# The cost that a build-time clock gives a matmul of the weight stream

## The chip, the cores and the metric

The kernel runs on one core of a Trainium2 chip. The metric is the device time of one execution, in microseconds. A core has five engines with queues of their own: TensorE (PE in the profile, its weight loads PEld), VectorE (DVE), ScalarE (ACT), GpSimd (POOL) and SyncE (SP), which here issues nearly all DMAs. An engine takes its instructions in the order in which the program has them, and waits where one of them needs what another engine has not done yet. The order of the instructions on each queue is therefore part of the program, and it is all that is changed here.

## The reference

One step of a layer of a hybrid decoder, for 256 prompt tokens and 8 sequences of 8 new tokens, 320 tokens in all, in float32:

```python
hn = rmsnorm(x, p['norm1'])
proj = hn @ p['w_in']                       # 2048 x 12752
y_s5 = s5_mixer(...)                        # diagonal state space, a scan over the tokens
y_rw = rwkv7_mixer(...)                     # a 64 x 64 state for each of 8 heads
y_gd = gdn_mixer(...)                       # gated delta rule, a 128 x 128 state for each of 8 heads
merged = (jax.nn.sigmoid(gt_s5) * (y_s5 @ p['w_br_s5'])
          + jax.nn.sigmoid(gt_rw) * (y_rw @ p['w_br_rwkv'])
          + jax.nn.sigmoid(gt_gd) * (y_gd @ p['w_br_gdn']))
x = x + merged @ p['w_out']
up = rmsnorm(x, p['norm2']) @ p['ffn_w_up'] # 2048 x 11264
up_c, n_ffn = causal_dwconv(up, ffn_conv, p['ffn_conv_w'])
gate, val = jnp.split(up_c + p['ffn_conv_b'], 2, axis=-1)
x = x + (jax.nn.silu(gate) * val) @ p['ffn_w_down']
```

The new states of the mixers and convolutions are outputs too, and x is normed once more at the end.

## The kernel before

*The weight stream.* All 320 tokens stand on the free axis, channels on the partitions. The weights come in 530 steps of 512 KB each (`plan`, line 2024): eight tiles of 128 x 128. Float32 accuracy is had from TensorE's faster format (F32R) by splitting: every weight tile w becomes a high part `whi` (ACT rounds it) and a low part `wlo` (DVE takes the difference), four tiles of 128 columns at a time (128 x 512), and the inputs are split in the same way. Each tile of a step is then three matmuls of 128 x 128 by 320 columns (`products`, line 554): whi with the input's high part, whi with its low part, wlo with its high part. This text calls them a triple. 530 steps are 4,240 triples, 12,720 weight matmuls. The splits are issued up to two steps ahead of their use.

*The tasks.* Everything else is written as generators, the tasks: first norm, S5, delta net (`gdn_main`, `gdn_prompt`, `gdn_sample`), RWKV (`rw_main`), the evacuation of PSUM banks, convolutions, gates. Their matmuls are ordinary float32 ones, most of them small: 64 columns, or 32 x 32 blocks in the inverses of triangular matrices (`tri_inverse`, line 1145, which sends blocks out to DRAM and back by DMA in another layout). A task issues one hop of instructions, then yields; its next hop may be issued when the inputs are held to be ready. S5 must end before the delta net begins, and the delta net before RWKV; RWKV must end before its branch's weights are due.

*What sets the order.* While the program is built, a `Clock` (line 112) keeps an estimated time for each engine. Each instruction is given a cost (`pe_cost` line 229, `dve_cost`, `act_cost`, `pool_cost`), and begins when its engine is free and its operands are ready, with a latency between engines (line 115). The chip does not see this clock; it only decides where instructions are put. After each triple, `poll` (line 531) lets tasks issue hops until the clock of PE has gone on by BURST = 500 ns; a hop in progress is not cut. `able` (line 522) says whether a task may go: its inputs must be ready at the time of PE's clock less 100 ns, free PSUM banks must be there, the DVE and ACT that it uses may be at most LEAD = 2100 ns ahead of PE's clock (double that for the first norm), and a task that uses PE must wait while the heat is negative. The heat (line 209) is a running balance: each matmul adds its columns (times 4 for float32, times its share of the 128 rows) and takes away PACE = 1.1 for each ns of PE's clock; it is capped at HEAT = 700. If no task may go, `split_some` (line 445) splits a part of the weights where ACT or DVE is not more than IDLE = 300 ns ahead of PE's clock. `finish` (line 542) lets tasks go on without the stream where a step needs their result.

The cost of a float32 matmul in the build-time clock is 5 + 1.667 ns for each of the larger of its columns and its weights' columns (line 233), and that of a pair of matmuls in different column groups is less. POOL's tensor_tensor of n elements a row costs 102 + 2.25 n ns (line 253), which the first norm uses to scale its 16 tiles (line 639).

Of the kernel before, what the change touches and what calls it, by code (L numbers as in the profile page):

```python
# [94 lines left out]
class Carve:  # L95
    """Pieces of one flat tile, one after the other."""
# [15 lines left out]
class Clock:  # L112
    """Estimates when each instruction runs, from the order of issue and what it reads and writes."""
# [24 lines left out]
    def after(self, eng, by, t):  # L138
        """When eng can go on after what another one did up to t."""
        return t if eng == by == "pe" or not t else t + self.LAT[by]  # L140

    def known(self, key):
        """What was done to a tile; a new one has to wait for those that had its place."""
        return self.mem.setdefault(key, [[(0, 1 << 20, 0, 1 << 40), self.freed, "dve", 0.0, "dve"]])
# [70 lines left out]
def run(ap):  # L215
    """Elements in a row of memory."""
    n = 1
    for s, c in reversed(ap.ap[ap.space != "DRAM":]):
        if s != n and c > 1:
            break  # L220
        n *= c
    return n
# [6 lines left out]
def pe_cost(name, outs, ins, a, k):  # L229
    n = free_size(outs[0])  # L230
    if ins[0].dtype == F32R:
        return 2.7 + n / 2.4
    return 5 + 1.667 * max(n, free_size(ins[0]) if name == "matmul" else ins[0].shape[0], 32)
# [28 lines left out]
class Engine:  # L262
    """An engine whose instructions the clock follows."""
# [36 lines left out]
class Task:  # L300
    """A generator that issues one hop of instructions after the other. It yields what the next hop waits for: a number of
    PSUM banks, or a condition."""
# [4 lines left out]
    def place(self):  # L307
        """Where it goes on."""
        g = self.gen
        while g.gi_yieldfrom is not None:  # L310
            g = g.gi_yieldfrom
        return g.gi_code, g.gi_frame.f_lineno


class Kernel:
# [43 lines left out]
    # ---- small helpers  # L359
# [9 lines left out]
    def bank(self, shape=(128, T)):  # L369
        """A free PSUM bank, as a tile of that shape."""  # L370
        i = self.spare.pop(0)
        n = int(np.prod(shape[1:]))
        a = self.banks[i][0:shape[0], 0:n]
        if len(shape) == 2:
            return a
        names = "abcd"[:len(shape) - 1]
        return a.rearrange("p (%s) -> p %s" % (" ".join(names), " ".join(names)), **dict(zip(names[1:], shape[2:])))
# [13 lines left out]
    def rstd_of(self, ms, out, tmp, twice=False):  # L391
        """1 / sqrt(ms + eps), with a Newton step after the tables; or -2 times that."""
        act, tt = self.nc.scalar.activation, self.nc.vector.tensor_tensor
        act(out, ms, AF.Ln, bias=self.eps)
        act(out, out, AF.Exp, scale=-0.5)
        tt(tmp, out, out, op=OP.mult)
        self.nc.vector.scalar_tensor_tensor(out=tmp, in0=ms, scalar=self.eps, in1=tmp, op0=OP.add, op1=OP.mult)
        if twice:
            self.nc.vector.scalar_tensor_tensor(out=out, in0=tmp, scalar=-3.0, in1=out, op0=OP.add, op1=OP.mult)
            return  # L400
        self.nc.vector.tensor_scalar(tmp, tmp, -0.5, 1.5, op0=OP.mult, op1=OP.add)
        tt(out, out, tmp, op=OP.mult)

    def halves(self):
        """Two parts of every tile of a matrix."""
        hi = self.mid.tile([128, KD, T], F32R, tag="hh", name="high")
        return [(hi[:, k], self.mid.tile([128, T], F32R, tag="hl%d" % k, name="low")) for k in range(KD)]

    # ---- the stream of weights
# [12 lines left out]
    def room(self):  # L422
        """How many parts of the weights may be split by now."""
        return self.PARTS * min(self.at + self.SPL_BUFS, len(self.steps))
# [20 lines left out]
    def split_some(self):  # L445
        """Splits a part where an engine has nothing to do."""
        c = self.clock.t
        if self.ns < self.nh and c["dve"] <= c["pe"] + self.IDLE:
            n, s = self.part(self.ns)
            if self.clock.written(self.split_t[n][0][:, s]) <= max(c["dve"], c["pe"]) + self.NEAR:  # L450
                self.split_low()
                return True
        if self.nh < min(self.room(), self.ns + self.AHEAD) and c["act"] <= c["pe"] + self.IDLE:
            self.split_high()
            return True
        return False

    def split_to(self, n):
        """Splits at least n parts."""
        while self.ns < min(n, self.PARTS * len(self.steps)):  # L460
            self.split_low()
        while self.nh < min(n + self.EARLY, self.room()):
            self.split_high()

    # ---- tasks beside it
# [19 lines left out]
    def spawn(self, gen, now=False, rank=2):  # L485
        """A task; those of low rank go first."""
        t = Task(gen, rank)
        self.tasks.insert(sum(u.rank <= rank for u in self.tasks), t)
        if now:
            self.hop(t)  # L490
        return t
# [8 lines left out]
    def par(self, *gens):  # L500
        """Generators side by side."""
        ts = [self.spawn(g) for g in gens]
        yield lambda: self.ended(*ts)

    def fetches(self, bufs, source):
        """Loads into a ring of buffers, each when what its buffer had is no longer needed."""
# [11 lines left out]
    def wait(self, *aps):  # L518
        """The next hop waits for these."""
        self.clock.end = max([self.clock.end] + [self.clock.written(a) for a in aps])  # L520
# [10 lines left out]
    def poll(self):  # L531
        """Lets the tasks issue what is ready to run."""
# [21 lines left out]
    def products(self, o, h, l, s, rhs, first, last):  # L554
        """Adds the products of some weight tiles, from number s on, with the pairs in rhs to the bank o."""
# [9 lines left out]
    # ---- first norm, input projection  # L565
# [40 lines left out]
    def prep(self, i):  # L606
        """Pair i of the input's tiles times the norm's weights, in two parts."""
# [3 lines left out]
    def norm1(self):  # L611
        """The factors of the tokens; the first columns are scaled by them afterwards, the others' input here."""
# [31 lines left out]
    def first_step(self, i):  # L644
        """Two tiles of the input for all of the first four columns."""
# [34 lines left out]
    def turn(self, ring, size, gen):  # L680
        """Starts a generator that uses the next of a ring's buffers, when the ones before have left it."""
# [7 lines left out]
    def evac(self, dst, p, r, parts=slice(None)):  # L689
        """A column of the projection out of PSUM; times the tokens' factors, if it came without."""  # L690
# [39 lines left out]
    # ---- gated delta net  # L730
# [52 lines left out]
    def head_norm(self, h):  # L783
        """Sums of a head's squares, key's and query's."""
# [7 lines left out]
    def gdn_main(self):  # L792
# [7 lines left out]
        # rows: one value per head and token  # L800
# [47 lines left out]
        # rows to all partitions, through DRAM  # L848
# [5 lines left out]
        # rows to tokens on partitions  # L854
# [17 lines left out]
        # value and key rows, tokens on partitions  # L872
# [22 lines left out]
        # products of keys with keys and queries inside a chunk  # L895
# [61 lines left out]
        # norm over the head, gate  # L957
# [27 lines left out]
    def gdn_prompt(self, s, ot, vt, kt, tk, yt, at, egl):  # L985
        """Chunk after chunk, the state in s."""
# [55 lines left out]
    def gdn_sample(self, shs, kqs, res, ot, vt, kt, tk, yt, at, egl):  # L1042
        """One state for each sequence and head, read once for the products and once for the update."""
# [64 lines left out]
        # both parts of keys and values, four blocks of rows for the four products  # L1108
# [36 lines left out]
    def tri_inverse(self, nt, halves, name, tw, tx, tt):  # L1145
        """(1 - n)^-1 in place of every 64 x 64 block n of nt (strictly upper; rows on partitions 64 hf + r, then groups of
        eight blocks); halves lists (hf, number of groups)."""
# [66 lines left out]
    # ---- S5  # L1214
    def pexp(self, x, out, new):
        """exp, to float32's accuracy."""
# [212 lines left out]
    def glu_step(self, ch):  # L1429
        """Columns 2 ch and 2 ch + 1 of the gate."""  # L1430
# [28 lines left out]
    # ---- RWKV  # L1459
# [39 lines left out]
    def rw_main(self):  # L1499
# [87 lines left out]
        # tokens on partitions  # L1587
# [37 lines left out]
        def solve(c, ws, first):  # L1625
            """uv of chunk c, from the states' part that first() adds."""
# [132 lines left out]
        # group norm, bonus, gate  # L1759
# [43 lines left out]
    # ---- branches and gates  # L1803
    def gate(self):
        """The next gate of the branches, or the next column of the input that the output projection adds to."""
# [53 lines left out]
    # ---- output projection, second norm's factors  # L1859
# [56 lines left out]
    # ---- feed forward  # L1916
# [26 lines left out]
    def ff_col(self, i, j, p):  # L1943
        """A column of the up projection: norm's factors, convolution; with the second of a pair, their product."""
# [29 lines left out]
    def down_step(self, g, cols, k0, n, last):  # L1974
        """n tiles from k0 on for each of the columns."""
# [32 lines left out]
    def end(self):  # L2008
        """The last norm; its factors come out times -2."""
# [62 lines left out]
def pack_w(w):  # L2072
    """Pieces of 8 x 128 rows by 128 columns."""
    k, c = w.shape
    return np.ascontiguousarray(w.reshape(k // 1024, 8, 128, c // 128, 128).transpose(3, 0, 2, 1, 4))


def pack_pairs(w):
    """Pieces of 4 x 128 rows by two times 128 columns."""
# [7 lines left out]
def device_inputs(inp):  # L2087
# [43 lines left out]
    def rw_cols(v):  # L2131
        """(..., RWKV columns) as 16 tiles of 128"""
# [39 lines left out]
def host_outputs(o):  # L2172
    """The device's arrays, channels first, in the reference's layouts."""
# [28 lines left out]
```

## Time and profile before

| what | us |
| --- | --- |
| runs before (device time) | 2127.69, 2132.31, 2140.75 |
| median | 2132.31 |
| profiled execution, from the first to the last instruction (span) | 2151.2 |
| PE busy | 2126.8 |
| DVE busy | 1368.1 |
| ACT busy | 1024.0 |
| POOL busy | 246.4 |
| mean granted TensorE clock | 0.973 |

The profiled execution has no other time of its own than its span; that lies 18.9 us above the median of the three runs. Durations below are those of the profiled execution.

How to read it: a row of the weight stream names the PSUM bank that is written and the operands, so `bank<-high,whi` is a matmul of the input's high part with a weight's high part. The name of the input tells the stage: xg and high are the first projection (from 5.6 and 72.4 us), yg, ys, yr the branches (from 892.5 us), high once more the output projection (from 1093.5 us), x2h and x2l the up projection (from 1206.2 us), hidh and hidl the down projection. All instructions are recorded under one line, L283, since one helper issues them; so one goes by the names. A float32 matmul leaves two records. The matmul records overlap: one begins before the one ahead of it has ended, so the distance of their starts, not their duration, is what one costs.

### The profile page before, as it was taken

What the parts mean: (1) busy time and instruction counts of PE and PEld (TensorE: products, weight loads), DVE (VectorE), ACT (ScalarE), POOL (GpSimd) and SP (SyncE); (2) the same over time, 40 slices, a digit from 0 to 9 for tenths busy, and PEclk for the clock granted to TensorE, in tenths of its full rate; (3) what the DMA queues carried; (4) which work ended last, traced back from release to release, by engine and by line L of the source; (5) the groups of instructions that cost most, each with busy time, mean ns of one, the idle gap of its engine ahead of it and who ended that gap; (6) DMA issues with size and microseconds to landing.
All of it is one profiled execution on the core that took longest, in us unless ns stands there. A gap on an engine that the chain in (4) does not pass through costs nothing.

```text
span 2151.2 us, 37239 instructions
## 1 busy us (share of the span) xinstructions
PE 2126.8 (99%) x14557; PEld 2042.6 (95%) x14557; DVE 1368.1 (64%) x2535; ACT 1024.0 (48%) x1932; POOL 246.4 (11%) x467
## 2 busy tenths in 40 slices
PE   8999999999999999999999999999999999999997
PEld 8999999999789999977999999999999999999997
DVE  7979898776238665714875666666644466666444
ACT  6666666653224765322444444444433344444443
POOL 2311101200000000000000122222200022222000
PEclk9999999999979999958999999999999999999999
DMA  6574555566317664623665544444444444444543
GB/s 230 193 250 146 160 171 172 161 205 198 134 45 254 226 204 135 201 83 92 212 200 177 162 147 151 149 152 148 153 150 147 150 153 148 147 151 151 165 149 106
DMA packets 131825, 351.05 MB, mean 163 GB/s; under 512 B 27024, under 2 KB 53184, under 8 KB 131392
## 3 DMA queue, kind: packets, MB, share of 16 engines
q1 hardware_dynamic: 130752, 345.56, 50.7%
q0 software_dynamic: 752, 3.10, 0.4%
q8 instruction: 114, 1.87, 0.3%
q14 instruction: 63, 0.52, 0.1%
q10 hardware_dynamic: 144, 0.01, 0.0%
HBM read 319.55 MB, written 29.06 MB: 162 GB/s over the span
## 4 chain that ended last, share of the span: by engine, by line
PE 97%; DVE 1%; DMA 1%; ACT 0%; issue 0%; SPq 0%; DVEq 0%; ACTq 0%
PE bank L283 97%; DVE low L283 0%; DVE wlo L283 0%; DMA x<-rdx 0%; DMA rdy<-triw 0%; DVE xf L283 0%; SPq L283 0%; DMA vec<-vec 0%; DMA x<-gdx 0%; ACT rstd L283 0%; DVE triw L283 0%; DVE squares L283 0%; DVE ev L283 0%; ACT whi L283 0%; DVE acc L283 0%
## 5 line engine op out<-in xcount | busy, mean ns | idle before, releaser
L283 ACT ACTIVATE whi<-wraw 128x512 fp32r<-128x512 f32 x1060 | 620.9, 624 | 765.1 <-issue 455.1
L283 DVE TENSOR_TENSOR wlo<-wraw,whi 128x512 fp32r<-128x512 f32 x1060 | 709.8, 694 | 382.7 <-ACT whi L283 373.3
L283 PE MATMUL bank<-high,whi 128*128 128x320 f32 x1728 | 550.5, 319 | 0.0
L283 PE MATMUL bank<-low,whi 128*128 128x320 f32 x1728 | 533.5, 309 | 0.0
L283 PE MATMUL bank<-high,wlo 128*128 128x320 f32 x1728 | 533.5, 309 | 0.0
L283 PE MATMUL bank<-x2h,whi 128*128 128x320 f32 x1408 | 435.3, 309 | 0.0
L283 PE MATMUL bank<-x2l,whi 128*128 128x320 f32 x1408 | 435.1, 309 | 0.0
L283 PE MATMUL bank<-x2h,wlo 128*128 128x320 f32 x1408 | 435.1, 309 | 0.0
L283 PEld LDWEIGHTS bank<-high,whi 128*128 128x128 f32 x1728 | 325.0, 188 | 23.0 <-issue 16.4
L283 PEld LDWEIGHTS bank<-low,whi 128*128 128x128 f32 x1728 | 325.6, 188 | 2.2
L283 PEld LDWEIGHTS bank<-high,wlo 128*128 128x128 f32 x1728 | 325.7, 188 | 0.0
L283 PEld LDWEIGHTS bank<-x2l,whi 128*128 128x128 f32 x1408 | 264.3, 188 | 0.1
L283 PEld LDWEIGHTS bank<-x2h,whi 128*128 128x128 f32 x1408 | 264.3, 188 | 0.1
L283 PEld LDWEIGHTS bank<-x2h,wlo 128*128 128x128 f32 x1408 | 264.3, 188 | 0.0
L283 PE MATMUL bank<-hidl,whi 128*128 128x320 f32 x704 | 216.5, 308 | 0.0
L283 PE MATMUL bank<-hidh,wlo 128*128 128x320 f32 x704 | 216.5, 307 | 0.0
L283 PE MATMUL bank<-hidh,whi 128*128 128x320 f32 x704 | 216.5, 307 | 0.0
L283 POOL COPY blk<-blk 128x62 f32<-128x62 f32 x88 | 63.5, 722 | 627.7 <-DVE blk L283 627.7
L283 PEld LDWEIGHTS bank<-hidh,whi 128*128 128x128 f32 x704 | 131.9, 187 | 0.0
L283 PEld LDWEIGHTS bank<-hidh,wlo 128*128 128x128 f32 x704 | 131.9, 187 | 0.0
L283 PEld LDWEIGHTS bank<-hidl,whi 128*128 128x128 f32 x704 | 131.9, 187 | 0.0
L283 DVE TENSOR_TENSOR blk<-bank,rstd 128x320 f32<-128x320 f32 x88 | 43.3, 492 | 104.0 <-PE bank L283 104.0
(332 smaller groups left out, 2301.3 us busy)
## 6 DMA issues: line engine op xcount, KB each, us to landing
wraw<-w_in SPq DMA_DIRECT2D x192, 512.0 KB, 4.0
wraw<-w_up SPq DMA_DIRECT2D x176, 512.0 KB, 3.6
wraw<-w_down SPq DMA_DIRECT2D x80, 512.0 KB, 3.6
wraw<-w_out SPq DMA_DIRECT2D x32, 512.0 KB, 3.4
shs<-gst SPq DMA_DIRECT2D x16, 512.0 KB, 3.9
wraw<-w_br_g SPq DMA_DIRECT2D x16, 512.0 KB, 3.7
gates<-ev SPq DMA_DIRECT2D x48, 160.0 KB, 1.8
gt<-gates SPq DMA_DIRECT2D x48, 160.0 KB, 4.2
```

Of the source, the lines that this page charges most:

```text
L283: return f(*a, **k)
```

## The change

One constant in the build-time clock's cost of TensorE's instructions. A matmul of the stream's format costs 13.2 ns beside its columns, where it cost 2.7 ns; for 320 columns 146.5 instead of 136.0. The costs of the float32 matmuls and of all other instructions stay. The rest of the diff takes out docstrings and comments and leaves every line where it was.

```diff
 def pe_cost(name, outs, ins, a, k):
     n = free_size(outs[0])
     if ins[0].dtype == F32R:
-        return 2.7 + n / 2.4
+        return 13.2 + n / 2.4
     return 5 + 1.667 * max(n, free_size(ins[0]) if name == "matmul" else ins[0].shape[0], 32)
```

The cost enters PE's estimated time (lines 206 to 210), and by it everything that compares with PE's clock: `begin`, `ended`, `able`, `poll`, `split_some`, and the heat. The instructions, their number, their operands and the buffers are the same; where the tasks' instructions and the splits stand in the queues is set anew by the program that builds the kernel.

## The prediction

> **What bounds the kernel now.** I read the profile page first (span, busy times, clock, chain, costliest groups), then the windows of some stretches, the waits, the chain in order of time, and the timeline of the two stages in which the clock falls.
>
> ```profile
> span 2151.2 us, 37239 instructions
> PE 2126.8 (99%) x14557; PEld 2042.6 (95%) x14557; DVE 1368.1 (64%) x2535; ACT 1024.0 (48%) x1932; POOL 246.4 (11%) x467
> ...
> PEclk9999999999979999958999999999999999999999
> ...
> PE 97%; DVE 1%; DMA 1%; ACT 0%; issue 0%; SPq 0%; DVEq 0%; ACTq 0%
> ...
> L283 ACT ACTIVATE whi<-wraw 128x512 fp32r<-128x512 f32 x1060 | 620.9, 624 | 765.1 <-issue 455.1
> L283 DVE TENSOR_TENSOR wlo<-wraw,whi 128x512 fp32r<-128x512 f32 x1060 | 709.8, 694 | 382.7 <-ACT whi L283 373.3
> ```
>
> TensorE (PE) carries 97% of the chain that ended last, and is busy for 99% of the span. No other engine is near: DVE 64%, ACT 48%. So the time is the sum of the matmuls at the granted clock, plus the little time in which PE waits. The clock row has two dips, near the middle.
>
> ```profile
> PE bank L283 <- ACT whi L283: 5.6, 1, 5.6
> PE bank L283 <- DVE wlo L283: 4.8, 3, 2.6
> PE bank L283 <- DMA x<-rdx: 0.7, 1, 0.7
> ```
>
> These are all the waits of PE that the profile shows: 11.1 us, of which 5.6 us is the first weight tile at the start. A better order can win back hardly anything here. What is left is the clock:
>
> ```profile
> 525.00:640.00 115.00, 114.89 (x864) 91.90 (x863) 28.45 (x74) 25.60 (x51) 0.54 (x1) 0.85 0.31 104
> ...
> 915.60:983.90 68.30, 68.30 (x540) 52.82 (x537) 9.54 (x18) 12.85 (x27) 1.46 (x5) 0.50 0.22 68
> 1080.00:2106.00 1026.00, 1026.00 (x6996) 1025.84 (x6995) 614.57 (x1057) 447.12 (x830) 158.73 (x270) 1.00 0.50 155
> ```
>
> In these rows the columns are: stretch, its length, busy time and count of PE, PEld, DVE, ACT, POOL, then granted clock. Half of the kernel, 1080 to 2106, runs at clock 1.00 with PE always busy: 1026.00 / 6996 = 146.7 ns per weight matmul. In the delta net's stage (525 to 640) the clock is 0.85, that is 2 x 0.15 x 115 = 34.5 us at half speed; in RWKV's stage 68.3 us stand at 0.50.
>
> **The change part by part.** One constant changes: line 232 gives a weight matmul of 320 columns 13.2 + 133.3 = 146.5 ns in the build-time clock instead of 2.7 + 133.3 = 136.0. The row above says 146.7, so the new figure is the right one. The instructions and their number stay. What moves is where the tasks' instructions are issued between the weight matmuls: while the build-time clock waits X for a task's input it now issues X / 146.5 weight matmuls rather than X / 136.0, 7.2% fewer.
>
> *The dense half, 1080 to 2106.* PE is never idle, tasks there issue almost no matmul, and DVE is busy 614.57 of 1026 us. Moving DVE and ACT work a few hundred ns earlier costs nothing; the cover is the weight tiles split up to two steps ahead. Taken as 0.
>
> *The two stages with small matmuls.* Does the new constant change how densely they lie? After every three weight matmuls (products, line 554) poll may issue tasks until 500 ns of PE time have been given out. If something is always ready, every triple is followed by one such hop, whatever a weight matmul is held to cost.
>
> ```profile
> 561.54 0.42 PE L283 MATMUL bank<-high,whi 128*128 128x320 f32 x1
> ...
> 562.09 0.33 PE L283 MATMUL bank<-kq,gs 128*128 128x64 f32 x2
> 562.35 0.43 PE L283 MATMUL bank<-at,vn 64*128 64x64 f32 x2
> 562.71 0.43 PE L283 MATMUL bank<-kq,gs 128*128 128x64 f32 x2
> 563.08 0.43 PE L283 MATMUL bank<-at,vn 64*128 64x64 f32 x2
> 563.44 0.41 PE L283 MATMUL bank<-high,whi 128*128 128x320 f32 x1
> ...
> 567.22 0.47 PE L283 MATMUL bank<-high,whi 128*128 128x320 f32 x1
> ...
> 570.32 0.63 PE L283 MATMUL bank<-high,whi 128*128 128x320 f32 x1
> ```
>
> A hop is 8 records here (an f32 matmul leaves two). The windows of the weight tiles alone, high parts first and low parts second, give the triples:
>
> ```profile
> 525.00:640.00 115.00, 40.82 (x139) 23.18 (x138) 11.54 (x18) 9.70 (x16) 0.85 0.31 104
> ...
> 525.00:640.00 115.00, 23.12 (x69) 14.70 (x69) 11.54 (x18) 0.85 0.31 104
> ```
>
> 139 + 69 = 208 weight matmuls are 69 triples; the other 864 - 208 = 656 records are 9.5 to each triple, one hop. So this stage is saturated, and so is RWKV's, where 540 records stand in 68.3 us. The second brake is the build-time heat (line 209): a triple earns 3 x (320 - 1.1 x 146.5) = 476 now, 511 before; the hop shown (costs 218 each, columns 256 and 128) earns 2 x 16 - 2 x 112 = -192. The balance stays positive, so this brake closes neither before nor after. Hence the density, and with it the half-clock time, stays about as it is. What half clock costs: the same triple and hop takes 563.44 - 561.54 = 1.90 us at full clock and 570.32 - 567.22 = 3.10 us at half; in RWKV's stage 3.57 against 2.11 us:
>
> ```profile
> 967.10 0.90 PE L283 MATMUL bank<-ys,whi 128*128 128x320 f32 x2
> ...
> 970.67 0.90 PE L283 MATMUL bank<-ys,whi 128*128 128x320 f32 x2
> ...
> 990.07 0.56 PE L283 MATMUL bank<-yg,whi 128*128 128x320 f32 x2
> ...
> 992.18 0.56 PE L283 MATMUL bank<-yg,whi 128*128 128x320 f32 x2
> ```
>
> With no half clock at all the stages would be 34.5 x (1 - 1.90/3.10) = 13.4 us and 68.3 x (1 - 2.11/3.57) = 27.9 us shorter: 41.3 us, the most that can be won. With the delta net's stage all at half clock its other 80.5 us would grow by 80.5 x (3.10/1.90 - 1) = 50.8 us. These are the ends for this term.
>
> *The waits for the triangular inverses.* Their blocks go out and come back by DMA, and the order covers that with weight matmuls.
>
> ```profile
> 520.84 0.34 SPq L283 DMA_DIRECT2D gates<-ev  x1
> ...
> 527.27 365.45 PE bank L283 x2521
> ...
> 897.95 0.32 SPq L283
> ...
> 905.32 6.47 DMA x<-rdx
> ...
> 911.84 1224.30 PE bank L283 x8468
> ```
>
> From the first SP issue of the chain to PE's going on are 6.4 us at the first and 13.9 us at the second, where PE already waited 0.7 us (row above). With 7.2% fewer weight matmuls as cover PE comes 0.5 and 1.0 us sooner and waits that much longer: +1.5 us, between 0 and, were the whole transfer bare, 6.47. Behind that wait stands the whole weight stream. The idle time comes just ahead of small matmuls, so I add one more stretch of 3.4 us (the dip's shortest unit, 34.5 us being some ten of them) at half clock in the delta net's stage: 3.4 x 0.39 = +1.3 us; its ends are the -41.3 and +50.8 above.
>
> *The first norm.* POOL scales 16 tiles while DVE splits them:
>
> ```profile
> 44.82 17.97 POOL L283 TENSOR_TENSOR x_sb<-x_sb,rstd 128x320 f32<-128x320 f32 x16 [29.89 <-ACT whi L283]
> ...
> L283 DVE SCALAR_TENSOR_TENSOR low<-x_sb,vec,high 128x320 fp32r<-128x320 f32 x14 | 13.8, 1028 | 0.0
> ```
>
> The build-time clock holds POOL's 16 at 822 ns each, 13.2 us, hence 97 weight matmuls before and 90 now. Seven fewer are 1.0 us less cover, and they need 0.6 of a low part of 0.69 us less: +0.6 us, between 0 and the 4.8 us that PE waits there now.
>
> *All other hops.* Outside these stretches 133 groups of small matmuls stand in the stream, from the first to the last of these rows:
>
> ```profile
> 127.89 0.73 PE L283 MATMUL bank<-csq,msk 128*32 128x320 f32 x4
> ...
> 1042.19 0.70 PE L283 MATMUL bank<-tn,mskr 128*128 128x320 f32 x2
> ```
>
> A typical wait ahead of one is an ACT pass and two DVE passes, 0.62 + 2 x 0.69 = 2.0 us (an estimate from the page's groups), so each comes up to 7.2%, 0.14 us, sooner against its input: at most 133 x 0.14 = 19 us. At the least 0; a gain is excluded, since PE shows no wait on a task's DVE or ACT work that could go. Tasks are only asked once a triple (0.44 us), which covers most of 0.14: I take a tenth, +1.9 us.
>
> *Sum.* 1.5 + 1.3 + 0.6 + 1.9 = +5.3 us. The profiled execution has a span of 2151.2 us and would come to 2156.5; it lies 18.9 us above the median of the timed runs, 2132.31. Against that median: 2137 us, +0.2%.
>
> **A rule against the change.** The rows give 146.7 ns per weight matmul. The Trainium skill, "TensorE: Matmul & The Clock Gate", section "Wait — 56ns, not 53.3ns?", puts back-to-back matmuls at N / 2.4 GHz + 2.5 ns, which would be 135.8 ns here, what the old constant holds. By it the new constant would make every hop too early, and the last term would stand at its end: 2132 + 19 + 3 = 2154 us. The trace disagrees by 11 ns.
>
> **The rivals.** (1) *Nothing moves that counts:* all hops stay covered, 2132 us. For it speaks that PE waits for no task now; against it that one DMA wait is already bare by 0.7 us.
> (2) *Slower, the clock:* the later DMA data at 527 us lets the clock fall at once, and the delta net's stage stays at half speed. For it: at 915.6 us the fall came right behind such a wait and lasted 68.3 us with PE busy throughout. Against it: in the same profile the first wait, at 527, was followed by full clock. All of the stage at half: 2132 + 51 = 2183 us. It decides from 21 us on, when 21 / 0.63 = 33 of the 80.5 us go over to half clock.
> (3) *Faster, the clock:* other neighbours for the small matmuls keep RWKV's stage at full speed. The span less 41.3 us is 2110 us, and no run can go lower by the clock alone; that is 22 us under the median. Against it: the stage is saturated, so its density hardly depends on the constant. The Trainium skill, same page, section "Why this matters for your kernels", says that the clock stays up if PE has no gaps over about 3 us. By that rule this rival would be sure, as the longest wait after the start is 2.6 us; the trace disagrees, with PE busy 68.30 of 68.30 us at clock 0.50.
>
> **How the numbers follow.** A measurement here can tell about 1%, 21 us, from no change. The small cost summed above: 0.59. Rival 1: 0.16; both end within 1%: 0.75. Rival 2 and late hops beyond 21 us: 0.15. Rival 3: 0.10. The time is that of the likeliest, 2137. The range takes in 19 us of late hops with the small terms (2154) and a small part of rival 2 above, and a 20 us gain of rival 3 below: 2112 to 2160, leaving out about 2 in 10.
>
> **What would show it.** In the changed profile: 146.7 ns per weight matmul in the dense half, as now; PE's wait for x<-rdx 1 to 2 us rather than 0.7, and one of about 0.5 us for x<-gdx; about 9.5 other records per triple in the delta net's stage; about 100 us at half clock in the two stages. A much larger or smaller half-clock time makes the prediction wrong, and so does a new wait of PE on DVE of over 10 us in the S5 stage, where DVE has the least room.

## The result

The changed kernel takes 2168.3 us in the median of four runs (2161.24 to 2173.6), against 2131.48 us before. The ratio is 1.0152, with a 95% interval from 1.0104 to 1.02: slower by about 1.5%, outside the predicted range. The same program once more, beside later kernels, gave 1.014 (1.0098 to 1.0182). The profiled execution is one of the four runs, 2161.24 us, with a span of 2159.5 us.

From the page of the changed kernel:

```profile
span 2159.5 us, 37235 instructions
PE 2115.3 (98%) x14557; PEld 2032.7 (94%) x14557; DVE 1360.2 (63%) x2535; ACT 1011.4 (47%) x1919; POOL 244.6 (11%) x467
...
PEclk9999999997899998999999999999999999999999
...
PE 84%; DVE 9%; DMA 3%; ACT 2%; issue 1%; SPq 0%; DVEq 0%; POOL 0%; ACTq 0%
```

The instructions are the same, and this execution even had less half-clock time than the profiled one of before (a mean clock of 0.980 against 0.973). But PE's share of the chain that ended last has fallen from 97% to 84%; DVE, DMA and ACT now stand in it. The chain in order of time was 130 pieces long and is now 799: again and again it leaves PE for the work that PE waits for. All waits of PE (us in total, times, longest):

```profile
PE bank L283 <- DVE wlo L283: 5.8, 4, 2.9
PE bank L283 <- ACT whi L283: 5.8, 1, 5.8
PE bank L283 <- DMA x<-rdx: 4.6, 1, 4.6
PE bank L283 <- DMA x<-gdx: 3.6, 1, 3.6
PE bank L283 <- DVE m L283: 3.0, 7, 0.9
PE bank L283 <- ACT csq L283: 2.3, 3, 1.1
PE bank L283 <- issue: 1.3, 1, 1.3
PE bank L283 <- ACT tp L283: 1.2, 1, 1.2
PE bank L283 <- DMA g<-rkv: 1.0, 1, 1.0
PE bank L283 <- DVE squares L283: 0.9, 1, 0.9
PE bank L283 <- DVE stacked L283: 0.7, 1, 0.7
```

They are 30.2 us, where they were 11.1: 19.1 us more. The first two, the start and the first norm, were there before, and so were 0.7 us of the wait for x<-rdx. The rest is new, and nearly all of it waits for the tasks: the two inverses, S5's output (m), the delta net's head norm (csq), RWKV's inputs.

The window of the delta net's stage, then two stretches at half clock, one at its start and one at the start of RWKV's small matmuls, then the dense half:

```profile
487.00:604.00 117.00, 114.23 (x854) 91.89 (x854) 27.54 (x72) 26.12 (x51) 0.54 (x1) 0.84 0.32 105
...
490.80:511.30 20.50, 20.50 (x181) 16.87 (x181) 1.99 (x3) 6.97 (x16) 0.00 (x0) 0.50 0.33 119
842.40:873.10 30.70, 28.09 (x309) 23.70 (x309) 2.16 (x4) 7.66 (x17) 1.47 (x5) 0.50 0.34 94
1090.00:2115.00 1025.00, 1025.00 (x6989) 1024.84 (x6988) 605.31 (x1053) 450.30 (x828) 158.59 (x270) 1.00 0.51 155
```

The dense half is what it was: 1025.00 / 6989 = 146.7 ns per weight matmul. The delta net's stage has 854 records in 117 us, against 864 in 115: nearly as dense, and at nearly the same clock, 0.84 against 0.85. What differs is where half clock begins. The timeline of PE (start, length, idle time before it in brackets) at the two inverses:

```profile
485.82 0.30 PE L283 MATMUL bank<-high,wlo 128*128 128x320 f32 x1
489.75 0.95 PE L283 MATMUL bank<-x,nt 32*32 32x32 f32 x32 [3.62 <-DMA x<-gdx]
...
840.14 0.31 PE L283 MATMUL bank<-high,wlo 128*128 128x320 f32 x1
845.01 1.91 PE L283 MATMUL bank<-x,gm 32*32 32x32 f32 x32 [4.56 <-DMA x<-rdx]
```

PE stands still for 3.62 us and 4.56 us with weight matmuls behind it in its own queue that need nothing. Half clock lasts from 490.8 to 511.3, right behind the first of these waits, and from 842.4 to 873.1, beginning within the second.

How much is waiting and how much is clock? Each run has its span and granted clock c, so its half-clock time is h = 2 (1 - c) x span. Lines fitted through the runs give span = 2102 + 0.42 h for before (81 runs, mean h 71 us) and 2125 + 0.41 h for the changed kernel (10 runs, mean h 91 us). So some 23 us are time that is there at full clock too, and 0.41 x 20 = 8 us are clock (the difference of the two means, 20 us, is uncertain by some 9, the 8 us by some 4). Below, the time at full clock is a kernel's mean span less 0.42 of its mean h.

### The profile page after: what moved, and what is told of

Same layout as the page of the kernel before. It is cut to its first block, busy times and chain, and to the rows that moved or that the text cites. A ratio compares the mean times of both kernels' runs of the same rounds, so it can differ in the third digit from the quotient of the medians.

```text
span 2159.5 us, 37235 instructions
## 1 busy us (share of the span) xinstructions
PE 2115.3 (98%) x14557; PEld 2032.7 (94%) x14557; DVE 1360.2 (63%) x2535; ACT 1011.4 (47%) x1919; POOL 244.6 (11%) x467
## 4 chain that ended last, share of the span: by engine, by line
PE 84%; DVE 9%; DMA 3%; ACT 2%; issue 1%; SPq 0%; DVEq 0%; POOL 0%; ACTq 0%
PE bank L283 84%; DVE wlo L283 3%; DVE m L283 1%; DVE t L283 1%; DVE conv L283 1%; ACT whi L283 1%; DVE bu L283 1%; DVE low L283 1%; DMA wraw<-w_in 0%; SPq L283 0%; DMA o_wkvs<-chain 0%; DMA x<-rdx 0%; DMA wraw<-w_u 0%; ACT tp L283 0%; DMA gdy<-triw 0%
## 5 line engine op out<-in xcount | busy, mean ns | idle before, releaser
L283 DVE TENSOR_TENSOR wlo<-wraw,whi 128x512 fp32r<-128x512 f32 x1060 | 701.1, 694 | 389.2 <-ACT whi L283 380.2
L283 PE MATMUL bank<-high,whi 128*128 128x320 f32 x1728 | 560.9, 325 | 0.0
```

Source lines behind the costliest of these rows:

```text
L283: return f(*a, **k)
```

## The experiments

Theory A: the loss is cover. The new constant puts fewer weight matmuls over every task chain, 7.2% by the arithmetic; the build-time clock holds these chains shorter than the chip takes, and the old, too small constant made up for that. Rival B: the loss is half-clock time that the small matmuls bring about by themselves. Rival C: another arrangement by chance, with no trend. The heat balance is no rival: in building the two programs it is below zero after 53 and 54 of 13,712 matmuls, and holds back no hop in either.

**More of the same.** The constant from 13.2 to 24.0:

```diff
-        return 13.2 + n / 2.4
+        return 24.0 + n / 2.4
```

> The constant at 24.0 ns, so that a weight matmul is held to take 157.3 ns: another 6.9% fewer weight matmuls over each chain. Theory A: the wait for x<-gdx grows to about 7 us, the one for x<-rdx to about 8 us, the waits of the S5 stage to more than double; the time rises by another 20 to 50 us, to 2190 to 2220. Rival B: as many triples and hops in the two saturated stages, so 2160 to 2180. Rival C (a true length is best, and the loss comes of a chance arrangement): 2130 to 2180, no trend.

Measured: 2197.67 us, ratio 1.0283 (1.024 to 1.0326). From its waits of PE:

```profile
PE bank L283 <- DVE m L283: 10.8, 12, 1.9
...
PE bank L283 <- ACT csq L283: 6.6, 5, 2.3
...
PE bank L283 <- DMA x<-rdx: 5.5, 1, 5.5
PE bank L283 <- DMA x<-gdx: 4.2, 1, 4.2
PE bank L283 <- DVE stacked L283: 3.9, 4, 1.0
```

The time goes on rising, and rival C falls. At full clock it is 2152 us, 27 more than the changed kernel's 2125, with only 10 us more at half clock (101 against 91), so Rival B does not explain it. S5's waits grew three times, but the two for the inverses by only 0.6 to 0.9 us where 3 to 4 were expected: the size of that step was missed. The weight matmuls over the two chains did fall, from 335 and 328 to 292 and 273, but the second chain itself took 49.8 us instead of 55.5, and within the first PE waited another 3.3 us for a weight's low part (wlo).

**Only the inverses.** The hop behind their DMAs is held back by 5 us of the build-time clock (in `tri_inverse`, behind the DMAs that bring the blocks back):

```diff
                 dma(out=x11[r, 0:n], in_=ap)
+        self.clock.end += 5000
         yield
```

> The changed kernel (13.2 ns), with the hop behind the two triangular inverses' DMAs held back by 5 us of the build-time clock. Theory A (cover): the chain from the first block's DMA out to the landing of the inverse's blocks takes 53.5 and 56.5 us in the trace of before; 7.2% fewer weight matmuls over all of it are 3.9 and 4.1 us less cover, which is what PE now waits (3.6 us for x<-gdx, 4.6 us for x<-rdx). Then both waits fall under 1 us here, and the time by 8 to 15 us, to 2153 to 2160. Rival B (clock): the half-clock stretches come of the small matmuls alone, not of the waits; then the waits go but the stretches behind them (20.5 and 30.7 us) stay, and the time falls by 8 us at the most.

Measured: 2148.02 us, ratio 1.0043 (1.001 to 1.0075), some 20 us less than the change's 2168, where 8 to 15 were expected. Neither x<-gdx nor x<-rdx stands among PE's waits any more. At full clock this kernel is 8 us shorter than the changed one (2117 against 2125), which is about the two waits; its mean half-clock time is 67 us against 91, which is worth another 10. In the profiled execution no half clock stands right behind the first inverse, where 20.5 us stood (the next stretch begins 63 us later), and 23.9 us instead of 30.7 behind the second. So a part of the half-clock time comes of the wait, as Theory A had it, and a part is there without it.

**Every hop.** `SLACK` from -100 to -600, so that a hop goes 600 ns after its inputs are held to be ready:

```diff
-    SLACK = -100
+    SLACK = -600
```

> The changed kernel, with every hop held back until its inputs are held to be ready for 600 ns rather than 100. Theory A: PE's waits on DVE and ACT work of the S5 stage (DVE m 3.0 us in 7 waits, 9.3 us at the weight loads, ACT csq 2.3 us) vanish, since each was under 1.4 us; the two waits for the inverses shrink by about 0.5 us at each link of their chains, to 2 to 4 us; the time falls by 8 to 15 us, to 2153 to 2160. Rival B: the S5 stage is at full clock anyway, so the time stays within 4 us of 2168.

Measured: 2146.11 us, ratio 1.0057 (1.0033 to 1.008). From its waits of PE:

```profile
PE bank L283 <- DVE m L283: 2.6, 6, 0.5
PE bank L283 <- DMA x<-gdx: 2.1, 1, 2.1
PE bank L283 <- DMA x<-rdx: 1.4, 1, 1.4
PE bank L283 <- ACT csq L283: 1.1, 2, 0.8
```

The time falls by more than was expected. The waits for S5's output did not vanish: 2.6 us remain of 3.0, though the longest is down to 0.5 us from 0.9, and those for the head norm are halved (1.1 us of 2.3). Over S5 lie even fewer weight matmuls than in the changed kernel, 1,584 against 1,615, so a hold for all tasks is not a hold for each; why is not shown.

**Both holds** together, 5 us and 600 ns:

> The changed kernel with both holds, 5 us behind the inverses' DMAs and 600 ns for every hop. Theory A: hardly a wait of PE is left besides the start and the first norm (under 15 us in all, 30.2 in the changed kernel); each hold alone gave some 20 us, but they share the inverses' waits, so 2130 to 2140, as before the change.

Measured: 2129.0 us, ratio 0.998 (0.9956 to 1.0004), as before the change, with the new constant kept. PE's waits are 15.3 us:

```profile
PE bank L283 <- ACT whi L283: 5.7, 1, 5.7
PE bank L283 <- DVE wlo L283: 5.2, 4, 1.9
PE bank L283 <- DVE m L283: 2.6, 6, 0.5
PE bank L283 <- DVE tp L283: 0.6, 1, 0.6
```

The mean granted clock of its 12 runs is 0.990 (44 us at half clock) against 0.979 in the changed kernel. So the constant does no harm once cover is given back by other means. But not all of the cover is back: at full clock this kernel takes 2107 us, 5 more than before's 2102, and its lower half-clock time (44 us against 71) makes up for that.

**One half of the timeline at a time.** The constant is 13.2 until S5 has ended and 2.7 from there on (s5_only), or the other way round (late_only):

```diff
-        return 13.2 + n / 2.4
+        return FIXED[0] + n / 2.4
...
         self.close("s5")
+        FIXED[0] = 2.7
```

> 13.2 ns until S5 has ended (first norm, first convolutions, S5), 2.7 ns from there on. Theory A: the waits of the S5 stage are as in the changed kernel (about 10 us more than before between 108 and 432 us), the ones for the two inverses as before (under 1 us): 2140 to 2150. Rival B (the delta net's and RWKV's stages decide): as before, 2127 to 2137.

> 2.7 ns until S5 has ended, 13.2 ns from there on, the other half of the split. Theory A: no more waits in the S5 stage than before, the waits for the two inverses at their size in the changed kernel (about 4 us each, both chains lie behind S5), with half-clock stretches behind them: 2145 to 2160, so that this part's loss and that of the S5 part (11 us by the medians) add up to about the whole, 34 us. Rival C (one chance arrangement): the two parts do not add up.

Measured: s5_only 2145.66 us, ratio 1.0048 (1.0022 to 1.0074), 11 us over before's 2134.43 beside it; late_only 2158.31 us, ratio 1.012 (1.0096 to 1.0144), 26 us over 2132.23. Together 37 us, where the whole change lost 37 us in the first comparison and 31 in the second: the parts add up. Against Rival B speaks the S5 part: the S5 stage is at full clock, and s5_only has no more half-clock time than before beside it (69 us against 75). Not all of its 11 us stand in S5, though: PE waits 2.0 us for x<-rdx, where under 1 was expected. In late_only half clock does count: 96 us against 70 beside it, worth 11 of its 26 us. PE's waits for the inverses are Theory A's there:

```profile
PE bank L286 <- DMA x<-rdx: 3.7, 1, 3.7
PE bank L286 <- DMA x<-gdx: 3.5, 1, 3.5
```

**The other direction.** The constant at -8.0:

```diff
-        return 2.7 + n / 2.4
+        return -8.0 + n / 2.4
```

> The constant at -8.0 ns, a weight matmul held to take 125.3 ns: 8.5% more weight matmuls over each chain than before. Theory A: no wait of PE on the inverses. But RWKV, which before ended 22 us ahead of the step that needs it, now ends behind it: the step waits, and RWKV's last hops run without the stream, for about 50 us, much of it at half clock: 2160 to 2200, with the waits at that place and not at the hops of S5. Rival (more cover is always better): 2125 to 2135.

Measured: 2171.66 us, ratio 1.0191 (1.0167 to 1.0216). More cover is not simply better. PE's idle times in the timeline behind 960 us begin with

```profile
988.79 2.60 PE L283 MATMUL bank<-x,gm 32*32 32x32 f32 x45 [23.16 <-DMA x<-rdx]
```

23.16 us of waiting for the second inverse. This is not a lack of cover by the constant: the stream has reached the branch that needs RWKV and has nothing left to lay over it (180 weight matmuls lie over the second chain, where 354 did). Weight matmuls of that branch begin at 1077.9 us, where they began at 1065.4 before. The late end was foreseen; that the wait for x<-rdx would carry it was not (no wait on the inverses was expected).

**Spreading the small matmuls.** In the changed kernel RWKV's last matmul stands 118.6 us ahead of the branch that needs it, in before 21.8. This kernel spends that room: SLACK -600, 3 us behind the inverses, float32 matmuls held 65 ns longer, PACE 1.4.

```diff
-    PACE, HEAT = 1.1, 700
+    PACE, HEAT = 1.4, 700
...
-    return 5 + 1.667 * max(
+    return 70 + 1.667 * max(
```

> The changed kernel, made to use the room it has before RWKV is due (it ends 32 steps ahead): every hop held 600 ns, 3 us more behind the inverses' DMAs, a float32 matmul held 65 ns longer, PACE 1.4 in place of 1.1, so that the heat balance goes negative and small matmuls lie further apart. Theory A with the clock: PE's waits under 20 us in all and half-clock time in the two stages under 40 us rather than 75: 2110 to 2125, less than both kernels. If the spread doesn't raise the clock: 2130 to 2140.

Measured: 2135.89 us, ratio 1.0028 (1.0006 to 1.005). The clock did what was expected, 0.994 in the mean, 27 us at half clock. The time did not. DVE m is back at 5.5 us among PE's waits: a longer float32 matmul slows PE in the build-time clock in S5 just as the change itself does. That is the smaller part. At full clock this kernel takes 17 us more than the one with both holds (2125 against 2107), and most of them stand in the two stages with small matmuls, where it hardly leaves full clock; why is not shown.

**Stage by stage.** mix_a has the old 2.7 and 100 ns until S5 has ended, then 13.2 with SLACK -600 and 3 us behind the inverses. mix_b and mix_c use the heat balance besides, after S5.

> Stage by stage, from what the runs so far gave: 2.7 ns and 100 ns until S5 has ended (its hops then wait for nothing), from there on 13.2 ns with both holds (600 ns for every hop, 3 us behind the inverses' DMAs). Theory A: PE's waits about 13 us in all, as before the change, without the bare wait for x<-rdx; half-clock time 30 to 60 us as with both holds: 2118 to 2126. If the S5 stage's arrangement hardly counts: 2129, as with both holds.

> As the last kernel, but after S5 a hop is held 400 ns, a float32 matmul held 35 ns longer and PACE 1.4, so that the heat balance goes negative and spreads the small matmuls; RWKV then ends two steps ahead of its due step. Theory A with the clock: half-clock time 10 to 30 us, waits as in the last kernel: 2108 to 2120. If RWKV comes late on the chip, PE waits ahead of the branch: over 2130.

> 2.7 ns with a hold of 300 ns until S5 has ended, then as with mix_b but 600 ns and PACE 1.3; RWKV ends seven steps ahead. Theory A with the clock: half-clock time between those of the two other mixes, 2110 to 2124.

> The changed kernel once more, beside the mixes: 2160 to 2174, with some 95 us at half clock against some 73 of before, and PE's waits at 30 us against 11.

Measured: mix_a 2125.38 us, ratio 0.9961 (0.9935 to 0.9987), 0.4% faster than before, as expected, and faster than the changed kernel. PE's waits with a task in them:

```profile
PE bank L286 <- DMA g<-rkv: 0.9, 1, 0.9
PE bank L286 <- DMA x<-rdx: 0.8, 1, 0.8
...
PE bank L286 <- ACT tp L286: 0.3, 1, 0.3
```

The mean clock is 0.991, 39 us at half clock against before's 67 beside it. That is what the gain comes of: at full clock mix_a takes 2106 us, no less than before's 2102. mix_b took 2144.2 us (1.0054, 1.0024 to 1.0085) and mix_c 2138.26 us (1.0019, 0.9987 to 1.0051): both missed, with 56 and 52 us at half clock, more than mix_a. After S5 the heat balance did not keep the clock up, and the runs don't show why it did in spread14. The changed kernel again: 2163.12 us, as expected.

## Why the prediction was wrong

*Which step failed.* The forecast of +5 us had four terms of one sign. The mechanism, less cover and so more waiting, was right; the sizes of three of the four were not, and most of all that of the term for all other hops. It named the gain as excluded, and that holds. Of its own signs, the wait for x<-rdx is 4.6 us where 1 to 2 were named, and the one for x<-gdx 3.6 where about 0.5 was.

*The inverses: +1.5 us was forecast, +7.5 us is there* (3.6 + 4.6 - 0.7). The prediction took 7.2% of the last legs, 6.4 and 13.9 us, which the chain of before happened to show. But the clock lays its cover over the whole stretch from the first block going out. In the trace of before that starts here:

```profile
473.67 1.95 SPq L283 DMA_DIRECT2D gdn<-nt  x3
...
855.30 2.58 SPq L283 DMA_DIRECT2D rdn<-gm  x2
```

To PE's going on at 527.27 and 911.84 that is 53.6 and 56.5 us, and 7.2% of them is 3.9 and 4.1 us. In the changed kernel the same chains take as long, 435.62 to 489.75 (54.1 us) and 789.55 to 845.01 (55.5 us), and the waits grew by 3.6 and by 4.6 - 0.7 = 3.9 us. The records show the cover that went: 362 and 354 weight matmuls lay over the two chains before, 335 and 328 in the changed kernel, and the 27 and 26 that are gone are 4.0 and 3.8 us. The chain of the slowest work shows where the path last changed engines, not how long the covered stretch is.

*All other hops: +1.9 us was forecast, some 13 us are there.* The prediction's upper end, 19 us, was nearer than the tenth that it took. It held 7.2% of the cover to go, a wait of 2.0 us to be typical, and one triple (0.44 us) to hide the loss. In fact more cover went. From the first matmul of the head norm to the last of S5, the windows of the high parts and then of the low parts are, first before and then in the changed kernel:

```profile
87.50:393.40 305.90, 275.09 (x1236) 205.51 (x1236) 104.91 (x156) 92.31 (x156) 1.00 0.56 177
87.50:393.40 305.90, 190.06 (x619) 115.82 (x618) 104.91 (x156) 1.00 0.56 177
85.10:363.10 278.00, 239.93 (x1076) 178.87 (x1076) 91.50 (x136) 80.71 (x136) 1.00 0.56 172
85.10:363.10 278.00, 165.51 (x539) 100.85 (x538) 91.50 (x136) 1.00 0.56 172
```

That is 1,855 weight matmuls and 1,615, 13% fewer. At 146.7 ns each they leave 33.8 and 41.1 us for the small matmuls and the waits: 7.3 us more. Why the cover fell by nearly twice 7.2% was not tested. A likely reason is that `able` also measures DVE against PE's clock: a step now lasts 3,516 ns there instead of 3,264, of which its two low parts take 1,204 on DVE, so DVE has 12% more time per step for the tasks' passes. S5's chains between two PE hops are longer: each output of S5 hangs on a row of DVE passes, two of them scans. In the changed kernel:

```profile
323.37 0.31 PE L283 MATMUL bank<-high,wlo 128*128 128x320 f32 x1
324.55 1.26 PE L283 MATMUL bank<-m,cc 128*32 128x320 f32 x4 [0.88 <-DVE m L283]
```

0.88 us of idle PE at one hop, where the prediction allowed 0.14. The waits other than for the inverses and the weights (DVE m, csq, issue, tp, g, squares, stacked) are 10.4 us in the table above, 6.6 of them between 100 and 432 us.

*The clock: +1.3 us was forecast, some 8 us are there.* That the stages' density would stay was right (854 records in 117 us against 864 in 115). That a longer wait would set half clock off was right as well, but it lasted 20.5 us, not 3.4. In the four traces in which PE waits over 3 us at both inverses (the changed kernel's two, const24, late_only), half clock follows each of the eight waits at once, for 20.5 to 47.8 us. The length does not follow the wait: 68.3 us in before and 71.7 us in s5_only stand behind waits of 0.7 and 2.0 us. In which stage the changed kernel's further 20 us lie is not shown, since the one trace of before is of an execution with unusually much half clock. Rival 2 had the place, the first inverse, and the mechanism; it did not decide alone, as the stage went back to full clock at 511.3 us. The Trainium skill, "TensorE: Matmul & The Clock Gate", section "Why this matters for your kernels", warns of gaps over about 3 us. The two gaps of 3.62 and 4.56 us agree with that; the later dips in the delta net's stage, between 518 and 573 us, have no gap: in the window shown above PE is idle for 2.77 us in all, the last part of the first gap.

*The first norm: +0.6 us was forecast.* The wait on DVE wlo went from 4.8 to 5.8 us: near enough.

*The dense half at 0* and the weight matmul's true length were right: 146.7 ns in both kernels. The rule that was set against the change gave 2154 us, nearer than the forecast, only because it took the upper end for the hops; its 135.8 ns the trace doesn't show.

*The sum.* Take from each stage's time 146.7 ns for every weight matmul in it, as for S5 above. What is left grows by 1.1 us ahead of the head norm's first matmul, 7.3 in the S5 stage, 6.5 from there to the first inverse, 6.9 from the delta net's last matmul to the second inverse, and not at all behind RWKV: some 22 us, where the lines through the runs gave 23. The inverses are 7.5 of them and the first norm 1.1, so the other hops are 13. Idle time of PE that the view counts makes up 18 of the 22; the other 4 are shorter delays (the weight loads alone wait 9.3 us in 24 places for DVE m, and never before the change). With 8 us of clock this gives 30 of the 31 to 37 us.

## What to carry to other kernels

An order planned with a model of the engines lives on the ratio of its costs. Correcting one of them to its true length can take margin that other chains lived on; give it back by name (a hold at the hop that waits longest) in the same edit. To price less cover, look at the whole stretch from where the covered chain leaves the engine to where the engine needs it, not at its last legs. A fixed share of that stretch fitted this change, but was worked out after its result, and missed the next step of the constant by 3 us at each inverse; counting the covering matmuls over the stretch in the new order is safer, and the chain's own length can change too.

## What was not expected of the hardware

Half-clock time has a price that is nearly the same from run to run: 0.42 us of span for each us of it in 81 runs of before, 0.41 in the changed kernel. And one program spreads widely, nearly by it alone: the runs of before lie between 2119.78 and 2152.23 us, but only some 1.4 us about their line. That is why the profiled execution of before, at 2151.2 us, was no fair measure of its median.
